# Small matmuls of an RWKV scan and a retention mixer, ordered by tile form and row half instead of in turns

## The chip, the cores and the metric

The kernel runs on one core of one Trainium2 chip. The metric is the device time of one execution in microseconds. The kernel before takes 2054.99 us (median of three runs, 2052.9 to 2055.63).

## The reference, cut to what matters

Two layers of a decoder work on a prompt of 512 tokens and on eight samples of four tokens each; both share the weights (`D_MODEL = 1024`). In each layer one large projection of the normalised input feeds four mixers and their gates; the mixers' results are merged, projected and added; then comes a feed-forward part. Two of the four mixers hold the change:

```python
# retention, chunks of 128 tokens, 4 heads of 64
s = jnp.einsum('bihd,bjhd->bhij', qb, kb) * dmask
o = jnp.einsum('bhij,bjhe->bihe', s, vb)
o = o + jnp.einsum('bihd,hi,bhde->bihe', qb, q_dec, S)
S = S * c_dec[None, :, None, None] + jnp.einsum('bjhd,hj,bjhe->bhde', kb, k_dec, vb)

# RWKV-7, 4 heads of 64, token by token
S = (S * wt[:, :, None, :]
     + jnp.einsum('bhij,bhj->bhi', S, at)[..., None] * bt[:, :, None, :]
     + vt[..., :, None] * kt[..., None, :])
y = jnp.einsum('bhij,bhj->bhi', S, rt)
```

For the samples the state comes in from memory, one per sample.

## The kernel before, in words

Features lie on the 128 partitions and the 544 tokens along the free axis, in two halves of 272. Nearly all weights stream from memory in units of 128 x 1024; each is split into a rounded part and a rest (ScalarE at line 109, VectorE at line 110), and each product is three matmuls (`mm3`, lines 129 to 131). These unit matmuls, 128 x 128 weights against 272 columns, are by far the largest part of the work of TensorE.

The mixers with small matmuls are generators (`rwkv`, `retention`). The program advances them by a step after each unit of weights (`tick`), so that their work stands between the unit matmuls. The code's order is not quite the order in which an engine runs its instructions: when the program is built, a scheduler puts each engine's instructions in order, by their place in the code among those whose inputs and buffers it holds ready. From then on each engine runs its list in order.

Heads of 64 features come in pairs: `p` is the pair, `q` the head within it. `par_rows(q)` are the partitions 0 to 63 or 64 to 127, and `kv_rows(q)` are the other half. The pieces that matter:

- *The scan of the prompt* (lines 587 to 628): 16 steps of 32 tokens in each layer, so 32 in all. A step makes `psG` (line 597), multiplies it by a triangular inverse (`ginv_sa`, line 577), and copies the result into the two halves of the state tile `Z`: `Z[0]` on VectorE (line 579), then `Z[1]` on ScalarE (line 580). Then come, for each of four pairs of `p` and `q`, a matmul into `psP` (line 604: 64 rows, 64 columns, with the row half `kv_rows(q)`) and one into `psY` (line 606: 128 rows, 64 columns). From `psP` VectorE and GpSimd make the next state (lines 612 to 621); every fourth step `psY` is copied out.
- *The samples of the scan* (lines 633 to 642): for each `p`, 16 matmuls of 64 x 64 weights against 8 columns into `psG0` (line 640), first the eight samples of one row half, then those of the other.
- *The retention* (from line 704, `def retention`), once for each `p` of each layer: scores of four chunks in two PSUM tiles, one for each `q` (line 720: 64 rows, 128 columns), masked on VectorE (line 723); products of keys and values (line 730) and their running sums `Sb` on VectorE; the output in `psO` (lines 742 and 744), where each chunk and head has one matmul from the masked scores (128 x 64) and, from the second chunk on, one from the state (64 x 64); and the samples (lines 765 and 767), where each `q` has one matmul from its scores (32 x 64) and eight of 64 x 64 from the samples' states.

PSUM tiles of these parts come from a pool of five banks (`psm`); the unit matmuls have three of their own.

Of the kernel before, what the change touches and what calls it, by code (L numbers as in the profile page):

```python
# [18 lines left out]
NB = 8  # L19
# [23 lines left out]
def tile_hybrid_step(ctx: ExitStack, tc: tile.TileContext, io: dict):  # L43
# [51 lines left out]

# [1 line left out]
    wloaded = {}  # L97
# [44 lines left out]

# [1 line left out]
    sgc = ZR(256)  # L144
# [13 lines left out]
    def ada_first(k):  # L158
        """feature tile k of the first norm's shift and scale; the four row groups sum every fourth 128 rows."""
        ps = PM()  # L160
        raw, sb = raws[k], sbs[:, 256 * k:256 * k + 256]
        for i in range(2):
            for kk in range(8):
                n = kk % 4
                PE.matmul(ps[32 * n:32 * n + 32, 128 * i:128 * i + 128], lhsT=sc[:, kk, :],
                          rhs=raw[:, 1024 * i + 128 * kk:1024 * i + 128 * kk + 128], start=(kk < 4), stop=(kk >= 4))
        S.copy(sb, ps[:, 0:256])
        yield
        for i in range(2):
            PE.matmul(ps[:, 256 + 9 * i:265 + 9 * i], lhsT=sb[:, 128 * i:128 * i + 128], rhs=cst[:, C_STK:C_STK + 9],  # L170
                      start=True, stop=True)
        V.tensor_tensor(
            out=mods[0].rearrange("p (s k) j -> p s k j", k=8)[:, 0:2, k, :],
            in0=ps[:, 256:274].rearrange("p (s j) -> p s j", s=2),
            in1=pars[0][:, P_BADA:P_BADA + 16].rearrange("p (s k) -> p s k", k=8)[:, :, k:k + 1].broadcast_to([128, 2, 9]),
            op=ADD)
        scales(0, (1,), slice(k, k + 1))
        yield

    def ada(l, sec, ns, load):  # L180
        """ns sections of the conditioning; a row group holds a fourth of their columns."""
        W = 256 * ns
        ps = PM()
        nxt = load(0)
        yield
        for k in range(8):
            raw = nxt
            if k < 7:
                nxt = load(k + 1)
            for n in range(4):  # L190
                PE.matmul(ps[32 * n:32 * n + 32, 0:W], lhsT=sc[:, k, :], rhs=raw[:, W * n:W * n + W], start=(k == 0), stop=(k == 7))  # L191
            yield
        sb = ZR(W)
        S.copy(sb, ps[:, 0:W])
        pt = PM()
        for q in range(2 * ns):
            PE.transpose(pt[:, q * 128:(q + 1) * 128], sb[:, q * 128:(q + 1) * 128], ident)
        V.tensor_tensor(
            out=mods[l][:, 8 * sec:8 * sec + 8 * ns, :].rearrange("p (n q) j -> p n q j", q=2 * ns),
            in0=pt[:, 0:W].rearrange("p (q n j) -> p n q j", q=2 * ns, n=4)[:, :, :, 0:9],  # L200
            in1=pars[l][:, P_BADA + 8 * sec:P_BADA + 8 * sec + 8 * ns].rearrange("p (n q) -> p n q", q=2 * ns).unsqueeze(3)
            .broadcast_to([128, 4, 2 * ns, 9]), op=ADD)
        scales(l, range(sec, sec + ns), slice(0, 8))
        yield
# [27 lines left out]

# [1 line left out]
    def xk(xt, k):  # L234
        return xt[k // 4][:, k % 4, :]

    def sum_sq(acc, x):
        """acc + x * x over the features seen so far."""
        sq = ZR(x.shape[1])
        S.activation(sq, x, AF.Square)  # L240
        if acc is None:
            return sq
        V.tensor_tensor(out=acc, in0=acc, in1=sq, op=ADD)
        return acc

    def rstd_of(accs):
        """(mean + eps) ** -0.5 of tokens, on every partition: taken with a token a partition, then spread."""
        n = HALF // 4
# [50 lines left out]
    def both_halves(run, norm):  # L299
        """eight output tiles, the first half's tokens and then the second's; a half's norm goes beside what follows."""  # L300
        ng = None
# [29 lines left out]

# [1 line left out]
    def par_rows(par):  # L333
# [5 lines left out]
    def ln_bones(src_halves, n, scale, bias, out, floor=None):  # L339
        """out = log(scale * blocksum(src) + bias) over 64-feature heads; exp_half makes it the sum's power -1/2."""  # L340
        for c0, c1 in ((0, HALF), (HALF, TOK)):
# [15 lines left out]
    def rwkv(l, za, zb, M, yD):  # L357
# [46 lines left out]
        def products(T):  # L404
            """the chunk's cumulative decays, and with them its scaled rows into LG and its scaled keys"""
            n = 128 if T < 4 else 32
# [33 lines left out]
        for T in range(5):  # L440
# [29 lines left out]
            yield  # L470
        # gate and bonus
        for p in range(2):
# [10 lines left out]
        yield  # L483
        # unit triangular inverses by substitution, a block (and row parity) a partition
        scr1 = drp.tile([64, 32, 32], F32, tag="scr1", name=nm("scr1"))
# [12 lines left out]
        nc.sync.dma_start(X, io["xinit"])  # L498
        # inverse of the samples' 4x4 blocks: (I + N)(I + N^2)
        psA2 = PM()  # L500
# [86 lines left out]
        for T in range(4):  # L587
            psY = PM()
            pY = psY[:, 0:256].rearrange("p (q x) -> p q x", q=2)
            for c in range(4):  # L590
# [10 lines left out]
                for p in range(2):  # L601
                    for q in range(2):
                        r = kv_rows(q)
                        PE.matmul(psP[par_rows(q), 64 * p:64 * p + 64], lhsT=BK[r, ch, p, :], rhs=Z[q][r, c % 2, p, :],  # L604
                                  start=True, stop=True)
                        PE.matmul(pY[par_rows(q), p, 32 * c:32 * c + 32], lhsT=Z[q][:, c % 2, p, :], rhs=LG[q][:, ch, p, 32:64],  # L606
                                  start=True, stop=True)
# [19 lines left out]
        G.dma_start(io["o_wkv_p"][l], Pn)  # L627
        # samples
        P0 = [ZR(512) for _ in range(2)]
# [4 lines left out]
        for p in range(2):  # L634
            if p:
                yield
            for q in range(2):
                r = par_rows(q)
                for b in range(NB):
                    PE.matmul(g0v[r, p, :, b, :], lhsT=P0[p][r, 64 * b:64 * b + 64],  # L640
# [34 lines left out]
        yield  # L675
        # group norm, bonus, gate
        rss = []
# [24 lines left out]

# [1 line left out]
    def retention(l, p, rt, M, yB):  # L704
# [10 lines left out]
        sms = []  # L715
        for q in range(2):
            r = par_rows(q)
            ps = PM()
            for T in range(4):
                PE.matmul(ps[:, 128 * T:128 * T + 128], lhsT=rt[r, 1, 128 * T:128 * T + 128],  # L720
                          rhs=rt[r, 0, 128 * T:128 * T + 128], start=True, stop=True)
            sm = ZR(512)
            V.tensor_tensor(out=sm.rearrange("j (T i) -> j T i", T=4), in0=ps.rearrange("j (T i) -> j T i", T=4),
# [14 lines left out]
        for T in range(4):  # L738
            for q in range(2):
                r = par_rows(q)  # L740
                oo = psO[r, 128 * T:128 * T + 128]
                PE.matmul(oo, lhsT=vt[:, T, r], rhs=sms[q][:, 128 * T:128 * T + 128], start=True, stop=(T == 0))  # L742
                if T:
                    PE.matmul(oo, lhsT=Sb[r, T, :], rhs=rt[r, 0, 128 * T:128 * T + 128], start=False, stop=True)  # L744
        S.copy(o[:, 0:SEQ], psO)
# [17 lines left out]
        for q in range(2):  # L763
            r = par_rows(q)
            PE.matmul(psO2[r, 0:32], lhsT=vks[32 * q:32 * q + 32, 0:64], rhs=sms_s[32 * q:32 * q + 32, :], start=True, stop=True)
            for b in range(NB):
                PE.matmul(psC[r, 4 * b:4 * b + 4], lhsT=S0[r, 64 * b:64 * b + 64], rhs=rt[r, 0, SEQ + 4 * b:SEQ + 4 * b + 4],
# [27 lines left out]
    def pad_evac(fn, dst, ps, half, pad):  # L795
        """write a half's tokens behind their past columns: fn(out, in)."""
        if half == 0:
# [7 lines left out]
    def first_units(k):  # L805
        """row tile k of the first three units, so that they run while the conditioning still arrives."""
        xh, xl = hh[k // 4][:, k % 4, :], hh[2 + k // 4][:, k % 4, :]
# [4 lines left out]

    # ================= program =================
    xs_dram = drp.tile([128, 8, TOK], F32, tag="xs", name="xs")
# [41 lines left out]
    for l in range(L):  # L856
# [80 lines left out]

# [1 line left out]
        yC = T4(F32R)  # L939
# [52 lines left out]

# [1 line left out]
        acc = []  # L994
        mix = None

        def gates(ys, first, last, hooks=()):
            """merge one branch; its projection runs a tile behind its gate, and hooks[m] after gate tile m."""
            nonlocal ui, mix
# [42 lines left out]

# [1 line left out]
        yA = T4(F32R)  # L1044
# [48 lines left out]

# [1 line left out]
        adv(rw, 2)  # L1095
# [48 lines left out]

# [1 line left out]
        wctx = ExitStack()  # L1146
# [26 lines left out]

# [1 line left out]
        fctx = ExitStack()  # L1175
# [109 lines left out]

# [1 line left out]
def _constants():  # L1287
# [197 lines left out]
```

## Time and profile before

| | |
|---|---|
| median of the timed runs | 2054.99 us (2052.9 to 2055.63, three runs) |
| span of the profiled execution | 2060.2 us |
| TensorE matmul busy (PE) | 98% of the span |
| TensorE weight load busy (PEld) | 92% |
| VectorE (DVE), ScalarE (ACT), GpSimd (POOL) busy | 51%, 40%, 15% |
| memory traffic | 227.23 MB, 110 GB/s on average |
| mean granted TensorE clock | 0.983 |

A line of the profile names a line of the code (L604), the engine, the operation, the tile written and the tiles read, and the form as rows x columns of the weights. Durations of matmuls are modelled and overlap each other, so that a group's busy time is no price; the chain of work that ended last gives each piece only the time that it adds. The granted clock is the share of TensorE's clock that the throttle let through. The profiled execution is one more execution beside the three timed ones.

### The profile page before, as it was taken

Reading aid. Unit: us, or ns where it says so; the run is one execution under the profiler, and the core shown is the slowest. Engines: PE = TensorE matmul, PEld = TensorE weight load, DVE = VectorE, ACT = ScalarE, POOL = GpSimd, SP = SyncE. Lnnn points to the kernel's source line nnn. Section 1 sums busy time; section 2 is a strip of 40 time slices with the busy share of each in tenths; the row PEclk is TensorE's granted clock in tenths of the full one; section 3 lists DMA queues with packets and bytes.
Section 4 is the critical chain, followed back from the end, with each engine's and each line's share of the span. In section 5 each row is a group of like instructions: output and inputs, shape, how many; then the busy total and the mean of one; then the engine's idle time right before and its main releaser. Section 6 shows DMA issues by size and latency. Waiting matters only on the chain.

```text
span 2060.2 us, 40148 instructions
## 1 busy us (share of the span) xinstructions
PE 2028.6 (98%) x16868; PEld 1897.2 (92%) x16868; DVE 1052.8 (51%) x2017; ACT 830.6 (40%) x1546; POOL 318.7 (15%) x589
## 2 busy tenths in 40 slices
PE   6999999999999999999999999999999999999998
PEld 5999988888999999999999999887899999999997
DVE  4465523353457553555663655333434666545565
ACT  5553322243336542434354533222533465333542
POOL 1110122212001220112202101222130012011210
PEclk9999999999999999999999999989999999999999
DMA  7224323232343443534322223123123322222221
GB/s 299 103 73 134 106 93 124 82 129 103 135 155 103 164 160 124 205 123 164 128 102 94 73 83 86 57 69 96 69 78 126 110 73 92 83 93 83 93 92 53
DMA packets 75557, 227.23 MB, mean 110 GB/s; under 512 B 20208, under 2 KB 23072, under 8 KB 73584
## 3 DMA queue, kind: packets, MB, share of 16 engines
q1 hardware_dynamic: 69872, 210.43, 29.9%
q0 software_dynamic: 3536, 11.53, 1.6%
q10 hardware_dynamic: 1968, 2.69, 0.5%
q8 instruction: 133, 2.18, 0.4%
q14 instruction: 48, 0.39, 0.1%
HBM read 213.33 MB, written 9.06 MB: 108 GB/s over the span
## 4 chain that ended last, share of the span: by engine, by line
PE 96%; DVE 2%; ACT 1%; DMA 0%; issue 0%; SPq 0%; DVEq 0%; ACTq 0%
PE pd L129 28%; PE pd L131 27%; PE pd L130 27%; PE pm L191 2%; PE pm L604 2%; PE pm L606 1%; PE pm L597 1%; PE pm L577 1%; DMA t<-in_wada 0%; PE pm L563 0%; PE pm L453 0%; PE pm L742 0%; PE pm L343 0%; PE pm L744 0%; DVE wlo L110 0%; PE pm L461 0%
## 5 line engine op out<-in xcount | busy, mean ns | idle before, releaser
L129 PE MATMUL pd<-t,whi 128*128 128x272 f32 x4200 | 1234.2, 294 | 5.2 <-ACT t L354 4.0
L131 PE MATMUL pd<-t,wlo 128*128 128x272 f32 x4200 | 1227.5, 292 | 0.0
L130 PE MATMUL pd<-t,whi 128*128 128x272 f32 x4200 | 1220.0, 291 | 0.6 <-DVE t L355 0.6
L129 PEld LDWEIGHTS pd<-t,whi 128*128 128x128 f32 x4200 | 795.9, 190 | 50.4 <-issue 34.7
L130 PEld LDWEIGHTS pd<-t,whi 128*128 128x128 f32 x4200 | 798.6, 190 | 7.5 <-issue 3.4
L131 PEld LDWEIGHTS pd<-t,wlo 128*128 128x128 f32 x4200 | 798.3, 190 | 4.4 <-issue 1.7
L110 DVE TENSOR_TENSOR wlo<-raw,whi 128x1024 fp32r<-128x1024 f32 x262 | 321.9, 1229 | 303.1 <-ACT whi L109 302.5
L109 ACT CAST whi<-raw 128x1024 fp32r<-128x1024 f32 x264 | 276.6, 1049 | 493.2 <-PE pd L130 456.8
L1196 POOL COPY off<-zr 128x18 f32<-128x18 f32 x88 | 77.0, 875 | 570.3 <-ACT zr L1194 570.3
L1016 DVE TENSOR_TENSOR zr<-pd,zr 128x272 f32<-128x272 f32 x96 | 41.6, 438 | 183.2 <-PE pd L131 183.0
L323 DVE SCALAR_TENSOR_TENSOR t<-pd,mod,t 128x272 f32<-128x272 f32 (+1 forms) x160 | 76.8, 482 | 112.1 <-PE pd L131 111.6
L1031 ACT ACTIVATE zr<-pd 128x272 f32<-128x272 f32 x128 | 50.4, 395 | 153.1 <-PE pd L131 148.8
L1194 ACT COPY zr<-pd 128x272 f32<-128x272 f32 (+2 forms) x264 | 72.7, 311 | 94.8 <-PE pd L131 94.8
L1017 POOL TENSOR_TENSOR t<-t,zr 128x272 f32<-128x272 f32 x64 | 73.2, 1160 | 218.3 <-DVE zr L1016 218.1
L945 DVE SCALAR_TENSOR_TENSOR zr<-zr,par,zr 128x560 f32<-128x560 f32 x92 | 73.5, 801 | 4.7 <-ACT zr L944 4.7
L946 DVE SCALAR_TENSOR_TENSOR zr<-zr,par,zr 128x560 f32<-128x560 f32 x92 | 73.5, 801 | 2.9
L944 ACT ACTIVATE zr<-zr,par 128x560 f32<-128x560 f32 x92 | 70.5, 766 | 7.6
L355 DVE TENSOR_TENSOR t<-zr,t 128x544 fp32r<-128x544 f32 (+1 forms) x96 | 54.0, 581 | 31.0 <-ACT t L354 30.1
L240 ACT ACTIVATE zr<-t 128x272 f32<-128x272 f32 (+1 forms) x72 | 32.1, 454 | 86.7 <-DVE t L323 54.5
L354 ACT CAST t<-zr 128x544 fp32r<-128x544 f32 (+1 forms) x96 | 48.9, 531 | 43.4 <-DVE zr L1207 42.0
L614 DVE TENSOR_TENSOR pt<-pm,pn 128x128 f32<-128x128 f32 x30 | 8.8, 292 | 70.7 <-PE pm L604 66.5
L604 PE MATMUL pm<-z,t 64*64 64x64 f32 x256 | 42.2, 246 | 0.0
(286 smaller groups left out, 1788.4 us busy)
## 6 DMA issues: line engine op xcount, KB each, us to landing
raw<-in_wst SPq DMA_DIRECT2D x276, 512.0 KB, 3.5
t<-in_wada SPq DMA_DIRECT2D x32, 1024.0 KB, 7.6
raw<-in_wada SPq DMA_DIRECT2D x32, 512.0 KB, 3.5
zr<-in_rope POOLq DMA_DIRECT2D x16, 272.0 KB, 3.2
t<-in_xT SPq DMA_DIRECT2D x4, 544.0 KB, 6.7
zr<-zr ACTq DMA_DIRECT2D x32, 68.0 KB, 4.3
t<-in_xT SPq DMA_DIRECT2D x2, 1088.0 KB, 8.3
xs<-t SPq DMA_DIRECT2D x2, 1088.0 KB, 4.4
```

Source lines behind the costliest of these rows:

```text
L109: S.copy(hi, raw)
L110: (G if (l, u) in ((0, 1), (0, 2)) else V).tensor_tensor(out=lo, in0=raw, in1=hi, op=SUB)
L129: PE.matmul(ps, lhsT=a, rhs=xh, start=first, stop=False)
L130: PE.matmul(ps, lhsT=a, rhs=xl, start=False, stop=False)
L131: PE.matmul(ps, lhsT=b, rhs=xh, start=False, stop=last)
L323: V.scalar_tensor_tensor(out=x[:, c0:c0 + npc], in0=ps[:, :npc], scalar=gate[:, m, 0:1], in1=x[:, c0:c0 + npc], op0=MUL, op1=ADD)
L604: PE.matmul(psP[par_rows(q), 64 * p:64 * p + 64], lhsT=BK[r, ch, p, :], rhs=Z[q][r, c % 2, p, :], start=True, stop=True)
L945: V.scalar_tensor_tensor(out=cv, in0=u[:, 1:561], scalar=wcol(1), in1=cv, op0=MUL, op1=ADD)
L946: V.scalar_tensor_tensor(out=cv, in0=u[:, 2:562], scalar=wcol(2), in1=cv, op0=MUL, op1=ADD)
L1017: (V if last else G).tensor_tensor(out=a[:, c0:c1], in0=a[:, c0:c1], in1=gs, op=ADD)
L1194: pad_evac(lambda o, i, sl: S.copy(o, i), u, ps, half, 2)
L1196: G.tensor_copy(off[:, 22 * s + j], u[:, 512:562].rearrange("p (x t) -> p x t", t=2)[:, 0:25:3, :])
```

## The change

Five groups of matmuls are put in another order. The instructions themselves stay the same, with their operands; comments and docstrings are taken out as well, line for line.

- Scan step: the four matmuls into `psP` come first, then the four into `psY`, instead of one of each in turns.
- Samples of the scan: the loop over the two row halves is now inside the loop over the samples.
- Scores of the retention: both PSUM tiles are taken at the start, and the two row halves take turns.
- Output of the retention: first all matmuls from the scores, then all from the state. Only the first chunk's matmul of each half has `start=True`; the others write into columns that nothing has been added to.
- Samples of the retention: first the two matmuls of 32 rows, then those of 64 rows with the row halves in turns.

```diff
@@ scan step
                         PE.matmul(psP[par_rows(q), 64 * p:64 * p + 64], lhsT=BK[r, ch, p, :], rhs=Z[q][r, c % 2, p, :],
                                   start=True, stop=True)
+                for p in range(2):
+                    for q in range(2):
                         PE.matmul(pY[par_rows(q), p, 32 * c:32 * c + 32], lhsT=Z[q][:, c % 2, p, :], rhs=LG[q][:, ch, p, 32:64],
                                   start=True, stop=True)
@@ samples of the scan
-            for q in range(2):
-                r = par_rows(q)
-                for b in range(NB):
+            for b in range(NB):
+                for q in range(2):
+                    r = par_rows(q)
                     PE.matmul(g0v[r, p, :, b, :], lhsT=P0[p][r, 64 * b:64 * b + 64],
...
@@ scores of the retention
-        for q in range(2):
-            r = par_rows(q)
-            ps = PM()
-            for T in range(4):
-                PE.matmul(ps[:, 128 * T:128 * T + 128], lhsT=rt[r, 1, 128 * T:128 * T + 128],
+        pss = [PM(), PM()]
+        for T in range(4):
+            for q in range(2):
+                r = par_rows(q)
+                PE.matmul(pss[q][:, 128 * T:128 * T + 128], lhsT=rt[r, 1, 128 * T:128 * T + 128],
                           rhs=rt[r, 0, 128 * T:128 * T + 128], start=True, stop=True)
+        for ps in pss:
             sm = ZR(512)
...
@@ output of the retention
         for T in range(4):
             for q in range(2):
                 r = par_rows(q)
-                oo = psO[r, 128 * T:128 * T + 128]
-                PE.matmul(oo, lhsT=vt[:, T, r], rhs=sms[q][:, 128 * T:128 * T + 128], start=True, stop=(T == 0))
-                if T:
-                    PE.matmul(oo, lhsT=Sb[r, T, :], rhs=rt[r, 0, 128 * T:128 * T + 128], start=False, stop=True)
+                PE.matmul(psO[r, 128 * T:128 * T + 128], lhsT=vt[:, T, r], rhs=sms[q][:, 128 * T:128 * T + 128],
+                          start=(T == 0), stop=(T == 0), skip_group_check=True)
+        for T in range(1, 4):
+            for q in range(2):
+                r = par_rows(q)
+                PE.matmul(psO[r, 128 * T:128 * T + 128], lhsT=Sb[r, T, :], rhs=rt[r, 0, 128 * T:128 * T + 128],
+                          start=False, stop=True, skip_group_check=True)
@@ samples of the retention
             PE.matmul(psO2[r, 0:32], lhsT=vks[32 * q:32 * q + 32, 0:64], rhs=sms_s[32 * q:32 * q + 32, :], start=True, stop=True)
-            for b in range(NB):
+        for b in range(NB):
+            for q in range(2):
+                r = par_rows(q)
                 PE.matmul(psC[r, 4 * b:4 * b + 4], lhsT=S0[r, 64 * b:64 * b + 64], rhs=rt[r, 0, SEQ + 4 * b:SEQ + 4 * b + 4],
```

## The prediction, made before the result was known

> **What bounds the kernel now.** First the page: span, busy time by engine, then the chain that ended last.
>
> ```profile
> span 2060.2 us, 40148 instructions
> ...
> PE 2028.6 (98%) x16868; PEld 1897.2 (92%) x16868; DVE 1052.8 (51%) x2017; ACT 830.6 (40%) x1546; POOL 318.7 (15%) x589
> ...
> PE 96%; DVE 2%; ACT 1%; DMA 0%; issue 0%; SPq 0%; DVEq 0%; ACTq 0%
> ```
>
> TensorE is busy nearly all the time, and 96% of the chain runs through it. So a microsecond taken out of TensorE's stream is worth about 0.96 us, as long as the stream has something else to run. A busy TensorE need not be a quick one, though: what one instruction costs is read from the chain in order of time, where each piece ends where the next begins. Here is one scan step of layer 0 (start, duration, what; every fp32 matmul leaves two records, so "x2" is one matmul of the code).
>
> ```profile
> 235.71 0.34 PE pm L597 x6
> ...
> 236.88 0.34 PE pm L577 x8
> ...
> 237.92 0.25 PE pm L604 x2
> 238.17 0.23 PE pm L606 x2
> 238.41 0.26 PE pm L197
> 238.67 0.26 PE pm L604 x2
> 238.92 0.23 PE pm L606 x2
> ```
>
> L577 runs eight records of one form in 0.34 us. L604 (a 64x64 tile) and L606 (128x64) alternate, and there two records already take 0.25 and 0.23 us, about three times as much a record. The rows of L604 and L606 in the list by form say how often:
>
> ```profile
> L604 PE MATMUL pm<-z,t 64*64 64x64 f32 x256 | 42.2, 246 | 0.0
> L606 PE MATMUL pm<-t,z 128*64 128x32 f32 x256 | 39.2, 236 | 0.0
> ```
>
> 256 records each are 128 matmuls each, four in each of 32 scan steps. What the same 64x64 form costs when its row halves take turns without another form between them, the chain shows at L453 and L461, 32 records each:
>
> ```profile
> 130.97 1.08 PE pm L453 x32
> 132.05 0.93 PE pm L461 x32
> ```
>
> L461 follows its own form: 0.93 / 32 = 0.029 us a record. L453 comes after a 128x128 form: 0.15 us more, the price of entering the form. These two numbers carry most of the sum. The other groups that are reordered, and the end of the scan's code beside them:
>
> ```profile
> 388.31 1.64 PE pm L720 x16
> ...
> 397.82 1.75 PE pm L640 x32
> ...
> 400.14 0.62 PE pm L730 x16
> 400.76 0.43 PE pm L742 x6
> 401.19 0.36 PE pm L744 x2
> 401.55 0.36 PE pm L742 x2
> ```
>
> L640 is the form of L461, but one row half at a time: 1.75 / 32 = 0.055 us a record, nearly twice L461's 0.029. L730 (128x64, the two column halves in turn) takes 0.62 us for 16.
>
> **The change, part by part.** No instruction is added or dropped, and no DMA is moved, so no queue of SP or POOL sees another order of its own work; what changes is the order of matmuls within TensorE's groups, and when their results are ready.
>
> *Scan (32 steps).* Before: 4 x (0.25 + 0.23) = 1.92 us a step. With four L604 and then four L606 in one piece each: 0.15 + 8 x 0.029 = 0.38 us, and about 0.36 us for eight of 128 rows (L577's eight take 0.34, half of L730's sixteen plus an entry 0.38): 0.74 us, 1.18 saved. I don't expect one piece each. In the step above a foreign matmul (L197) stands behind the first L604 and L606: the second L604 needs the scan state's other half, which is copied a little later. In the changed order the first L604 is followed by one that isn't ready; the first L606 is ready, then comes the filler, then the remaining three L604 and three L606. L597 already shows such a split, with its x6 in 0.34 us. So: 0.25 + 0.23 + 0.34 + 0.34 = 1.16 us, 0.76 saved, x 32 = 24.3 us. Bounds: 37.8 us (32 x 1.18) in whole groups, and nothing if the instructions end up alternating anyway.
>
> *Retention output (four times: two layers, two head pairs).* L742 has 16 records, L744 twelve. Before: 0.43 + 5 x 0.36 + 6 x 0.36 = 4.39 us. After: 16 in the six's pace (0.43 / 6 = 0.07, of which the last is unpaired) 1.0 to 1.15 us, twelve with an entry 0.8 to 1.0 us; 1.9 together. 2.5 saved, x 4 = 10.0 us. L744 also waits for running sums of the state on VectorE; behind all of L742 it is later, so these are readier than before.
>
> *Sample loop of the scan (L640, four times).* 1.75 becomes 0.15 + 32 x 0.029 = 1.08 us: 0.67 x 4 = 2.7 us.
>
> *Sample loop of the retention (L767, four times).* For the first head pair of a layer it is cut in two by L765, another form:
>
> ```profile
> 420.11 0.23 PE pm L765 x2
> 420.34 1.02 PE pm L767 x16
> 421.36 0.23 PE pm L765 x2
> 421.58 1.17 PE pm L767 x16
> ```
>
> 2.65 us become 0.23 + 1.08 = 1.31, 1.3 saved, twice; where it is in one piece I take L640's 0.67, twice. Together 3.9 us.
>
> *Scores (L720, four times).* 16 records at 0.103 us, one half after the other. Side by side eight pairs at about 0.107 and an entry: 1.0 us; 0.6 x 4 = 2.4 us. Both PSUM banks must now be free before the first matmul; the row shows all sixteen in one piece, so both were held then too, and I price this at nothing (a late bank would put unit matmuls in front, which are due anyway). The masks on VectorE start some 0.5 us later for the first half; TensorE has unit matmuls to run meanwhile.
>
> Sum of the matmuls: 24.3 + 10.0 + 2.7 + 3.9 + 2.4 = 43.3 us.
>
> *The clock.* Four stretches hold all these groups, and in each the granted clock (the figure behind the five engines' busy times) is below 1:
>
> ```profile
> 230.00:390.00 160.00, 159.94 (x1404) 133.50 (x1403) 53.42 (x112) 42.41 (x101) 35.17 (x58) 0.96 0.26 87
> 390.00:500.00 110.00, 109.96 (x923) 92.33 (x924) 45.73 (x74) 45.47 (x75) 21.83 (x25) 0.97 0.36 122
> 1260.00:1408.00 148.00, 148.00 (x1245) 126.04 (x1245) 47.84 (x98) 36.56 (x87) 35.38 (x54) 0.93 0.19 62
> 1408.00:1515.00 107.00, 105.99 (x841) 90.83 (x840) 42.16 (x69) 42.97 (x71) 24.00 (x28) 0.94 0.23 78
> ```
>
> 0.04 x 160 + 0.03 x 110 + 0.07 x 148 + 0.06 x 107 = 26.5 us of clock are lost there. In slices of 3.41 us:
>
> ```profile
> 282.39:285.80 3.41, 3.38 (x29) 2.40 (x29) 0.29 (x1) 0.89 (x3) 0.80 (x2) 1.00 0.78 286
> 285.80:289.21 3.41, 3.41 (x16) 3.35 (x16) 2.18 (x4) 0.65 (x1) 0.51 (x1) 0.50 0.07 26
> 289.21:292.62 3.41, 3.41 (x29) 3.41 (x29) 0.00 (x0) 0.40 (x1) 0.00 (x0) 1.00 0.43 154
> ```
>
> The slice that starts at 282.39 holds a whole run of L604 and L606 and hardly a large matmul; the next one is granted half the clock and gets 16 matmuls instead of 29, a loss of 13 x 0.12 = 1.6 us. The scan's two stretches lose 16.8 us, about ten such slices. There are 32 steps and only some ten slow slices, so a run of L604 and L606 is near the edge of what brings one. With the run 0.76 us shorter, six more large matmuls (3.41 / 29 = 0.12 us each) fit into its slice, and most should stay on the full side. I take 15 of the 26.5 us back. Ends: 25 (all of it), and 5 lost if the denser small groups bring three new slow slices.
>
> The Trainium skill ("TensorE: Matmul & The Clock Gate", Part 1) says that the gate halves the clock after an idle window of about 3.4 us. The length agrees with the slices here; that the window must be idle does not, for TensorE stands as busy 3.38 of 3.41 us before the slow slice. Read by busy time the rule would leave this term at nothing and the time at 2013.
>
> *Cover.* VectorE and ScalarE are busy for a third of the scan's stretches or less and DMA for about a quarter, so weights keep up with a TensorE that is 10% quicker there. For what ends on other engines I take the chain's 96%: (43.3 + 15) x 0.96 = 56 us. The profiled execution's span of 2060.2 us becomes 2004; it lies 5.2 us above the median of the three timed runs, 2054.99, which becomes **1999**.
>
> **The rivals.**
>
> *Whole groups.* If the state's other half counts as ready in time, the scan saves 37.8 instead of 24.3 us and more of the clock returns (20): (43.3 + 13.5 + 20) x 0.96 = 74 us, 1981. For it: the state's second half is copied within 0.58 us of the first (rows below), little more than the 0.48 that the first two matmuls take. Against: the filler in the step above.
>
> *The clock stays.* The gate counts something that the shorter runs don't change; busy time is the same in slow and full slices. 43.3 x 0.96 = 42 us, 2013.
>
> *Row halves don't overlap into one bank.* L604, L640, L744 and L767 write both row halves into one PSUM bank. If these run in turn, at 0.055 us a record (L744, with twice the columns, at 0.103): scan 0.25 + 0.23 + 0.48 + 0.34 = 1.30, 19.8 saved; L640 nothing; L767 1.3; L744 and L742 2.0 x 4 = 8; L720, on two banks, 2.4. With 10 of clock 41.5 x 0.96 = 40 us, 2015. L453 and L461 write one bank from both row halves too, and their 0.029 speaks against it. The Trainium skill ("TensorEngine Tiling (Array Packing)", Restrictions and Gotchas, Gotcha 1) states that different row tiles can't use the same bank at once; in this trace they do, on disjoint partitions.
>
> *The order isn't followed.* Engine order is planned when the program is built, by what is ready, and the scan's matmuls become ready one by one. If the scan alternates as before, only the loops whose inputs all stand ready gain: 19.0 + 5 of clock, x 0.96 = 23 us, 2032.
>
> *Slower: TensorE stalls within the step.* TensorE takes its stream in order. If the plan puts the four L604 close together on a modelled time at which the second half isn't copied yet, TensorE stands, with L606 and all unit matmuls queued behind. The copies:
>
> ```profile
> 258.93 0.29 DVE L579 COPY z<-pm 32x128 f32<-32x128 f32 x1 [0.95 <-PE pm L577]
> ...
> 259.25 0.26 ACT L580 COPY z<-pm 32x128 f32<-32x128 f32 x1 [0.83 <-DVE z L579]
> ```
>
> From the first copy's start to the second's end are 0.58 us, 18.6 over 32 steps. That alone doesn't eat 43.3. It does if each stall also brings a slow slice: 1.6 us in each of the 22 steps that have none now, 35 us; 43.3 - 18.6 - 35 = -10, 2065. It turns the sign once some 20 of the 32 steps pay 0.58 + 1.6. Against: L604 rarely waits now, since fillers stand ahead of it, and these stay.
>
> **How the numbers follow.** Forecast 0.50, whole groups 0.17, clock stays 0.17, no overlap 0.04, order not followed 0.08, stall 0.025, nothing measurable 0.015. About 0.2% (4 us) can be told from no change; every case but the last two is faster by more. The range, 1972 to 2027: its lower end is whole groups with all the clock ((43.3 + 13.5 + 25) x 0.96 = 79, and some 4 us for entries that the fillers need no more), its upper end the scan at half its saving and 2 us of clock lost ((12.2 + 19.0 - 2) x 0.96 = 28); outside lie the order not followed and the last two.
>
> **What would show it.** In the chain of the changed kernel L604 and L606 should stand as x2, x2, then x6, x6 (or x8, x8) with under 1.2 us a step; L742 x16 and L744 x12 in pieces, L640 and L767 x32 at 1.1 us, L720 x16 at 1.0. The granted clock of the four stretches should be 0.98 or more. Wrong would be: 0.055 us a record in alternating halves; the same number of slow slices; idle time ahead of L604 put down to the copies of L579 and L580; or a chain that leaves TensorE for more than 4%.

## The result, and the profile after

The changed kernel takes 2000.16 us (median of four runs, 1997.68 to 2001.29) against 2055.31 us before (four runs, 2052.9 to 2065.68). The ratio is 0.9719, with a 95% interval from 0.9691 to 0.9746. The forecast was 1999 us, in a range from 1972 to 2027.

The page of the kernel after: span, busy time by engine, and the chain by engine.

```profile
span 1995.9 us, 40151 instructions
...
PE 1962.4 (98%) x16868; PEld 1850.0 (93%) x16868; DVE 1047.5 (52%) x2017; ACT 829.4 (42%) x1546; POOL 318.8 (16%) x589
...
PE 95%; DVE 2%; ACT 1%; DMA 1%; issue 0%; ACTq 0%; SPq 0%; DVEq 0%
```

TensorE is as full as before, with the same 16868 matmul records; the span is shorter by what they took. The same scan step as in the prediction, in the chain of the kernel after (start, duration, what; L604 has kept its line, L606 is now L608):

```profile
239.12 0.26 PE pm L604 x2
239.37 0.23 PE pm L608 x2
239.60 0.26 PE pm L197
239.86 0.37 PE pm L604 x6
240.23 0.35 PE pm L608 x6
240.58 0.26 PE pm L197
```

The pieces are x2, x2, the filler, x6, x6, as forecast: 0.26 + 0.23 + 0.37 + 0.35 = 1.21 us instead of 1.92. In the trace 30 of the 32 steps have this form; the other two have whole groups.

The retention and the sample loops in the chain of the kernel after (L722 are the scores, L642 the samples of the scan, L744 and L749 the output; L771 and L775 the samples of the retention):

```profile
372.64 1.09 PE pm L722 x16
...
381.58 1.03 PE pm L642 x32
...
383.18 0.62 PE pm L733 x16
383.80 0.88 PE pm L744 x16
384.67 0.80 PE pm L749 x12
385.48 0.88 PE pm L642 x32
```

```profile
399.91 0.23 PE pm L771 x4
400.14 1.03 PE pm L775 x32
```

The output takes 0.88 + 0.80 = 1.68 us instead of 4.39. The second L642 has no entry to pay, since it follows L749, which has its form. And the four stretches that hold these groups, with the granted clock behind the five busy times:

```profile
230.00:372.00 142.00, 140.13 (x1392) 118.30 (x1391) 52.66 (x112) 41.14 (x99) 33.09 (x54) 1.00 0.30 100
372.00:465.00 93.00, 92.96 (x895) 79.57 (x894) 40.41 (x69) 40.34 (x70) 22.75 (x27) 1.00 0.40 134
1227.00:1358.00 131.00, 131.00 (x1305) 113.75 (x1303) 49.12 (x107) 40.22 (x98) 35.41 (x54) 1.00 0.23 70
1358.00:1465.00 107.00, 105.49 (x945) 94.96 (x944) 47.09 (x77) 50.17 (x81) 26.97 (x30) 0.98 0.28 92
```

Before they stood at 0.96, 0.97, 0.93 and 0.94. In this execution a single slow slice (one at half clock) is left in them, behind the retention's samples at 1441 us.

Single executions differ by the clock that they were granted, so times are also compared at one clock here. The kernel before ran 27 times beside the experiments, from 2050.76 us at a mean granted clock of 0.989 to 2071.06 at 0.980. A straight line through the 27 gives 1.86 us for each 0.001 of clock, and 2044.2 us at 0.993, the kernel after's usual clock. Their median is 2058.9 us at 0.985. So of the roughly 58 us between the kernels in these runs, about 44 are there at equal clock and about 15 are clock (8 x 1.86). This is an estimate, for none of the 27 executions had 0.993, and the line is drawn on past them.

### The profile page after: what moved, and what is told of

Read it like the earlier page. It is cut to its first block, busy times and chain, and to the rows that moved or that the text cites. A ratio compares the mean times of both kernels' runs of the same rounds, so it can differ in the third digit from the quotient of the medians.

```text
span 1995.9 us, 40151 instructions
## 1 busy us (share of the span) xinstructions
PE 1962.4 (98%) x16868; PEld 1850.0 (93%) x16868; DVE 1047.5 (52%) x2017; ACT 829.4 (42%) x1546; POOL 318.8 (16%) x589
## 4 chain that ended last, share of the span: by engine, by line
PE 95%; DVE 2%; ACT 1%; DMA 1%; issue 0%; ACTq 0%; SPq 0%; DVEq 0%
PE pd L129 28%; PE pd L131 27%; PE pd L130 27%; PE pm L191 2%; PE pm L604 1%; PE pm L608 1%; PE pm L597 1%; PE pm L577 1%; DMA t<-in_wada 1%; PE pm L453 0%; PE pm L563 0%; PE pm L343 0%; PE pm L165 0%; PE pm L461 0%; PE pm L672 0%
## 5 line engine op out<-in xcount | busy, mean ns | idle before, releaser
L1200 POOL COPY zr<-sff 128x16 f32<-128x16 f32 x88 | 41.0, 476 | 0.7 <-DMA sff<-in_s_ffn 0.4
L1211 ACT ACTIVATE zr<-zr 128x560 f32<-128x560 f32 x44 | 29.6, 672 | 24.9 <-DVE zr L954 24.9
```

## The experiments

**The scan step alone, and all but the scan step.** The first is the kernel before with this edit, the second the kernel after without it:

```diff
                                   start=True, stop=True)
+                for p in range(2):
+                    for q in range(2):
                         PE.matmul(pY[par_rows(q), p, 32 * c:32 * c + 32], lhsT=Z[q][:, c % 2, p, :], rhs=LG[q][:, ch, p, 32:64],
```

> The kernel before with the scan step alone reordered (four L604, then four L606). Theory (order costs TensorE time by itself, the clock is a smaller share): the two lines' own time falls from 63.5 to about 38 us as in the changed kernel, and of the ten slow slices in the scan's stretches hardly one stays; the slow slices of the sample stages (near 422, 1426 and 1446 us in the profile before) stay. 26 plus 6 to 10 us, 2020 to 2025 us. Rival (the gain is the clock's above all, and either part alone lifts it): the time comes within 10 us of the changed kernel, 2000 to 2010.

> The changed kernel with the scan step's order of before, so that only the retention's output and scores and the two sample loops are reordered. Theory: 18.5 us of matmul time plus 3 to 6 us of clock in the sample stages, 2030 to 2035 us; the slow slices in the scan's stretches stay. The savings of this run and of the scan alone add up to the whole within 5 us. Rival (the clock's part is common to both): they add up to clearly more or less than 55 us.

The scan alone took 2031.42 us (ratio 0.9856, 0.9826 to 0.9886), the rest alone 2025.38 us (0.9837, 0.9804 to 0.987). Both expected times missed, in opposite directions: the scan brought less and the rest more. Against the kernel before beside them (2060.33 us) they save 28.9 and 35.0 us, 63.9 together. The whole change saved 55.2 in its own runs and 61.4 in a later set, so this alone doesn't settle whether the parts add within 5 us. Moved along the line to a clock of 0.993 they are 2019.1 and 2026.3 us, savings of 25.1 and 17.9 us, which add up to 43.0 against the whole change's 44. What differed is the clock, a median of 0.9865 with the scan alone and 0.9935 with the rest alone. How far the line carries is shown by the next pair of profiles. The rival of the first run, 2000 to 2010 us, falls.

**Where the slow slices lie.** The kernel before and the scan alone were each profiled again, unchanged.

> The kernel before, unchanged, for a second look at where its slow slices lie. Theory (the slices depend on how the free-running 3.41 us grid falls on the stages): again 30 to 50 us at half clock between the first and the last microseconds, but at other steps of the scan; those of the sample stages come back at the same stages. Rival (they are tied to the instructions): the same ten or so places as in the first profile.

> The scan step alone reordered, for a second look at its slow slices. Theory A (each stage's slices depend on that stage's own matmuls): few in the scan's stretches (under 14 us at half clock), 20 us or more in the sample stages. Theory B (the first profile's split between the stages was chance): more in the scan than in the sample stages.

They took 2058.65 and 2026.03 us. The second execution of the scan alone had a clock of 0.993 and is still 7 us above the 2019.1 that the line gives, so the line is no better than that for this kernel. The four stretches of the kernel before, second profile, and then of the scan alone, second profile:

```profile
230.00:388.00 158.00, 156.98 (x1393) 130.59 (x1392) 52.75 (x111) 42.34 (x101) 34.28 (x56) 0.97 0.26 86
388.00:500.00 112.00, 111.95 (x943) 94.08 (x939) 45.99 (x76) 46.49 (x76) 23.23 (x27) 0.97 0.36 120
1255.00:1406.00 151.00, 151.00 (x1315) 128.47 (x1309) 51.10 (x106) 40.85 (x98) 37.02 (x57) 0.95 0.19 61
1406.00:1515.00 109.00, 107.87 (x853) 92.79 (x853) 43.39 (x71) 45.59 (x72) 22.91 (x25) 0.94 0.27 84
```

```profile
230.00:374.00 144.00, 141.63 (x1405) 119.51 (x1406) 52.74 (x112) 42.38 (x102) 34.16 (x56) 1.00 0.30 98
374.00:480.00 106.00, 105.95 (x895) 88.21 (x894) 43.59 (x71) 40.61 (x69) 22.09 (x26) 0.97 0.35 119
1240.00:1373.00 133.00, 132.25 (x1310) 114.50 (x1309) 49.62 (x108) 41.40 (x99) 35.81 (x55) 1.00 0.22 69
1373.00:1480.00 107.00, 105.67 (x842) 91.24 (x841) 42.10 (x69) 42.91 (x71) 23.93 (x27) 0.94 0.24 80
```

With the scan reordered its own two stretches stand at 1.00 and those of the samples stay at 0.97 and 0.94, so theory A holds. The first profile of the scan alone has 10.2 us at half clock in the scan's stretches, at one place, and 27.3 in the others. In the kernel before, the scan's part varies: 34.1 us at half clock in the first profile, 23.9 in the second. Of these 23.9 us, 17.1 stand in the same steps as in the first profile (one slice at 285 us, four in a row from 1351 and 1347 us) and the rest in others, so that neither the theory nor its rival holds as it stands. The samples' part is 20.5 us in both and stands at the same three stages. The profile of the rest alone, its execution with the lowest clock (0.990), shows the mirror image:

```profile
232.00:388.00 156.00, 155.17 (x1390) 129.16 (x1390) 52.50 (x111) 42.04 (x101) 33.71 (x55) 0.98 0.26 87
388.00:480.00 92.00, 91.56 (x886) 78.41 (x883) 40.96 (x67) 39.02 (x67) 21.25 (x26) 1.00 0.41 135
1242.00:1396.00 154.00, 154.00 (x1319) 130.89 (x1319) 52.69 (x108) 41.86 (x99) 35.67 (x56) 0.93 0.18 60
1396.00:1485.00 89.00, 87.67 (x815) 77.55 (x814) 40.68 (x68) 39.94 (x67) 21.40 (x25) 1.00 0.28 92
```

Each stage's slow slices come from that stage's own matmuls, with one exception. The scan alone has 10.2 us at half clock from 344.9 us on, the kernel after's second run 10.2 us from 342.9 us on, and these follow a pause of TensorE. Here are that run's slice with the pause (3.41 us long, TensorE busy for 1.86) and the one behind it, at half clock, and the wait that made the pause:

```profile
339.48:342.89 3.41, 1.86 (x21) 1.34 (x21) 2.89 (x6) 0.45 (x2) 0.81 (x1) 1.00 0.44 154
342.89:346.31 3.42, 3.42 (x27) 2.82 (x28) 0.29 (x1) 0.26 (x1) 0.00 (x0) 0.50 0.76 219
```

```profile
PE pm L597 <- DVE z L622: 1.6, 1, 1.6
```

Every kernel with the quicker scan waits near this place (1.6 to 3.0 us idle in one piece); the kernel before doesn't, or waits 1.0 us. In the four profiles where one slice held 1.5 us or more of the wait (scan alone, kernel after again, and two of the variants below, the output in turns and the halves in blocks), slow slices followed. In the first profile of the kernel after and the second of the scan alone a border of the slices, counted on from their slow ones, cuts the wait (1.24 and 0.56, 1.22 and 0.78 us), and none followed. Between these it went either way: none behind 1.49 us with the late half first at both lines, one behind 1.23 us with the late half first (both below).

The profiles also give a second estimate of what the order alone saves. A microsecond at half clock costs at most half a microsecond; with that taken off the spans for the four stretches' slow slices, the kernel before stands at 2032.9 and 2034.3 us, the scan alone at 2011.1 and 2014.0, the rest alone at 2017.3, and the kernel after at 1994.2 and 1992.1. These are savings of 21 and 16 us for the parts and 40 for the whole. They add within 3 us, which is also what two profiles of one kernel differ by.

**As many microseconds of small matmuls, but in dense groups.** This tells whether length or alternation brings the slow slices. The products are the same, written over again:

```diff
-                for p in range(2):
+                for p in [0, 1] * 3:
                     for q in range(2):
                         r = kv_rows(q)
                         PE.matmul(psP[par_rows(q), 64 * p:64 * p + 64], ...
-                for p in range(2):
+                for p in [0, 1] * 2:
                     for q in range(2):
                         PE.matmul(pY[par_rows(q), p, 32 * c:32 * c + 32], ...
```

> The changed kernel, but each scan step issues its four L604 three times and its four L608 twice (the same products written over again), so that the small matmuls of a step last about as long as before, 1.9 us, without alternating forms. 24 more records a step at 0.029 us: 0.70 us, 22 us over 32 steps. Theory C (a slice turns slow when too much of it goes to small matmuls, whatever their order): the slow slices of the scan come back, 7 to 14 us more, 2029 to 2037 us. Theory D (it is the alternating forms, in which the array stands empty, that bring them; dense small matmuls count as work): the granted clock stays at 0.993, 2020 to 2025 us.

It took 2019.6 us (ratio 0.9826, 0.9795 to 0.9857), at a median clock of 0.995. One step in its chain, and the scan's two stretches:

```profile
258.55 0.25 PE pm L604 x2
258.81 0.23 PE pm L608 x2
259.04 0.55 PE pm L191 x2
259.59 0.84 PE pm L604 x22
260.42 0.58 PE pm L608 x14
```

```profile
230.00:382.00 152.00, 150.15 (x1777) 128.47 (x1777) 51.28 (x110) 42.34 (x101) 34.60 (x56) 1.00 0.28 89
1236.00:1381.00 145.00, 145.00 (x1704) 126.76 (x1704) 50.37 (x109) 41.68 (x99) 35.83 (x56) 1.00 0.22 65
```

A step spends 0.25 + 0.23 + 0.84 + 0.58 = 1.90 us on small matmuls, as before the change, and no slice of the scan is slow. Theory D holds, for all four executions' clocks (0.993 to 0.996, against 0.979 to 0.989 of the kernel before) and for the time, which lies just under its 2020 us: in the scan dense small matmuls keep the clock, and it is not the length of a step's small matmuls that loses it. Most of the alternation is what the run takes away; that something else goes with it (how much of the array works in each microsecond, say) is not ruled out.

**The order of the halves in the scan.** First blocks of two instead of turns:

```diff
-                for p in range(2):
-                    for q in range(2):
+                for q in range(2):
+                    for p in range(2):
```

> The changed kernel, but in the scan step both L604 of one row half come first and then both of the other, and the same for the two column halves of L608 (this also lets the ready half run first, so pieces of x4, x4, filler, x4, x4). Theory (taking turns between halves counts beside the form): a step's own time goes from 1.21 to about 1.44 us, 7 us more over 32 steps, 2005 to 2010 us. Rival (only the change of form counts, halves in turns bring nothing): no slower than the changed kernel, 1997 to 2002.

It took 1991.97 us (0.9666, 0.9637 to 0.9695), 8 us less than the kernel after instead of 7 more: the expectation failed. A step of it in order of time, TensorE alone (durations overlap; the next start counts):

```profile
247.70 0.46 PE L604 MATMUL pm<-z,t 64*64 64x64 f32 x8
248.09 0.43 PE L608 MATMUL pm<-t,z 128*64 128x32 f32 x8
248.45 0.39 PE L131 MATMUL pd<-t,wlo 128*128 128x272 f32 x1
```

The groups came out whole: while both L604 of the half that is ready run, the other becomes ready, and 26 of 32 steps have x8, x8. And the whole groups take 0.39 + 0.36 = 0.75 us here (up to 0.84 in other steps), not much more than in turns (0.73, below), though the halves stand in blocks of two. So at this length the order of the halves hardly counts, and most of the gain is the entry into the form that no longer falls due twice: all matmuls of L604 and L608 together take 29.8 us where the kernel after has 37.7.

Then turns, but beginning with the half that is copied last:

```diff
-                    for q in range(2):
+                    for q in (1, 0):
```

> The changed kernel, but in the scan step the row half whose state is copied last comes first in both groups, so that all eight matmuls are ready when the first is and the groups stay whole (x8, x8). Theory: a step's own time goes from 1.21 to 0.73 us in some 29 steps, 14 us, and the filler needs no entry of its own, 3 to 5 us more: 1981 to 1986 us. Rival (the first matmul now waits for the second copy, 0.58 us after the first, and TensorE stands): idle time ahead of L604 of up to 0.5 us a step eats the gain, 1995 to 2005 us.

It took 1981.86 us (0.9613, 0.9584 to 0.9642), as the theory said. All 32 steps have whole groups. TensorE's waits for the second copy are 1.2 us in one place, as the list of waits shows:

```profile
PE pm L604 <- ACT z L580: 1.2, 1, 1.2
```

Done at L597 as well:

> As the run with the late half first, and L597 in that order too, so that its four matmuls are ready together. Some 13 steps no longer split L597: 0.2 us of entry each, and a filler's entry of 0.2: 3 to 5 us less than with the late half first, 1976 to 1980 us. Rival (L597's filler only moves ahead of it, and TensorE waits for the second half): the same, 1981 to 1984.

It took 1979.43 us (0.9623, 0.9599 to 0.9646). A step in its chain:

```profile
237.58 0.38 PE pm L604 x8
237.95 0.35 PE pm L608 x8
```

The step's 0.73 us are nearly the prediction's price of whole groups, 0.74. Against the run before it the gain is 2.4 us between two separate sets of runs on two chips (1978.4 to 1980.1 against 1979.2 to 1983.1): under the expected 3 to 5, and not told apart from nothing. Only six steps fewer split L597 (three against nine), not some 13.

**Parts of the rest, undone.** With the kernel after run again beside them.

```diff
# the sample loops: halves in blocks of eight samples (the same at L775)
-            for b in range(NB):
-                for q in range(2):
-                    r = par_rows(q)
+            for q in range(2):
+                r = par_rows(q)
+                for b in range(NB):
```

> The changed kernel, but in the two sample loops (L642, L775) the eight samples of one row half come first and then those of the other; the forms still stand together. Theory (in a long group the row halves must take turns to overlap): each of the eight loops goes from 1.03 back to 1.75 us, 5.8 us, and the slow slices that stood behind L767 come back in part, up to 6 us: 2006 to 2012 us. Rival (as in the scan's blocks of two, the order of the halves hardly counts): within 2 us of the changed kernel.

> The changed kernel with the retention's output alone as before (the two forms in turns). Theory: 2.7 us more in each of four places, 10.8 us, and some of the slow slices of that stage, up to 5 us: 2010 to 2016 us. Rival (the output's matmuls wait for VectorE's sums and masks anyway): under 5 us, 2000 to 2005.

> The changed kernel once more, on the same chip as the two runs beside it: 1997 to 2002 us, no more than two slow slices between the first 40 and the last 30 us.

The kernel after took 1998.7 us again (1996.24 to 2004.0). Its profile has three slow slices in a row from 343 us on, one more than expected; they are those behind the pause of TensorE shown above. The sample loops in blocks took 2012.57 us (2003.95 to 2017.51), just past the expected range; at a clock of 0.993 it is 2007.8, some 5 to 8 us above the kernel after, and the rest is clock (0.987 to 0.994 from run to run, where the kernel after beside it had 0.992 to 0.997). Two of the loops in its chain, which stood at 1.03 and 0.88 us in turns:

```profile
381.54 1.75 PE pm L642 x32
...
386.15 1.60 PE pm L642 x32
```

Here the form stays the same, and only the halves differ. The profile of this run has one slow slice behind an L642 and one behind an L775, where the kernel after's second run has none. So slow slices also come behind loops without alternating forms, whose small matmuls run one row half at a time. Nor are groups in turns wholly free of them: the kernel after's only one in the four stretches, in its first profile, follows a slice with an L775 in turns, and so do those of the repeated products (466 us) and of the late half at L597 too (446 and 1422 us). The output in turns of forms took 2010.82 us, 12 us more than the kernel after, as expected, at a clock of 0.993.

## Why the prediction was right, point by point

*The bound.* TensorE's stream did set the time: the order's 40 to 44 us, by the two estimates, are the sum of the matmul terms (43.3) at nearly full worth. Whether 0.96 was the right factor is finer than they can tell.

*The matmul terms.* Scan 1.21 us a step where 1.16 was put: 1.92 - 1.21 = 0.71, x 32 = 22.7 us for 24.3. Output 4.39 - 1.68 = 2.71, x 4 = 10.8 for 10.0. L642 saves 0.72 for 0.67, in both loops (1.75 to 1.03, and 1.60 to 0.88 against the halves in blocks). The retention's samples 2.65 - 1.26 = 1.39 for 1.3 where L765 had cut them. Scores 1.64 - 1.09 = 0.55 for 0.6. The split into x2, x2, x6, x6 was forecast from the filler in the step of before, and it came.

*The clock.* The way was right, and the size roughly: 15 of the 26.5 us were to come back. The line gives about 15, but 11 for the result's own medians (55.2 less 44), and the profiles' half-clock time gives 26 for the two first profiles (54.6 and 3.4 us). So the close agreement of the total has luck in it, and two of the reasons were wrong. The prediction put 16.8 of the loss into the scan from one profile; the scan's slices vary from execution to execution, and it is the rest that brings back most in the timed runs (a median of 0.9935 with the rest alone; 0.986 or 0.987 with the scan alone, and 0.993 once). Why the scan alone lies so low in most of them is open in part: its two profiles place 37.5 and 20.5 us at half clock in the four stretches, and 10.2 of the difference follow the pause at 341 us. And it said that the run of small matmuls, being shorter, leaves room for six more large ones in its slice. The repeated products show that this isn't what counts: the run was as long as before and the clock stayed. What failed is that step's mechanism, not its sum.

The Trainium skill ("TensorE: Matmul & The Clock Gate", Part 1) says that the clock is set by how busy TensorE has been recently. If busy is read from the profile, the pause near 340 us agrees (1.86 of 3.41 us busy, then half clock) and the scan of before does not: alternating and dense groups look equally busy in the profile, and in the scan only the first lose the clock. What the gate counts stays open; no run here measures it.

*The rivals.* Whole groups did not come, but two other orders of the same loop brought them. Beginning with the late half gains what the rival said (1981 forecast, 1981.86 measured); blocks of halves, with whole groups in 26 steps, reach 1991.97. That the clock stays falls with the four stretches. Row halves do overlap into one bank: L642 in turns takes 1.03 us for 32 records that take 1.75 in blocks. The order was followed. The stall didn't come; even with the late half first the matmuls' own waits for the copy are 1.2 us.

*Cover.* VectorE, ScalarE and the weight stream kept up but for one place, which the prediction does not name. From 330 to 342.7 us the chain of the kernel after leaves TensorE:

```profile
330.09 0.73 ACT whi L109
...
334.00 5.06 DMA zr<-zr
...
342.07 0.50 DVE z L622
...
342.70 0.27 PE pm L597 x2
```

A DMA for the retention's inputs comes first, then VectorE's sum that needs it (line 1135), then the scan's next state (L622), for which TensorE, with unit matmuls until then, waits 1.8 us. With the late half first its waits for L622 are 3.2 us. This is what a still quicker scan meets, and, in the executions where the pause falls into one slice, it costs clock as well.

## What to carry to other kernels

Read the price of small matmuls from the chain, per record and per change of form, and compare it with a place in the same kernel where the form stays: here two records cost 0.25 us after another form and 0.06 after their own. Put matmuls of one form together, begin with the operand that is ready last, so that the whole group is ready when it starts, and let row halves take turns where the group is long. Then look at the granted clock of the stretch before and after, because here alternating forms cost a second time there, and look for pauses that the quicker stream has opened.

## What the runs showed of the hardware that was not expected

- What taking turns between row halves brings depends on the length of the group: in groups of four matmuls, blocks of two cost 0.75 to 0.84 us for a step's two groups against 0.73 in turns, while in groups of sixteen, blocks of eight cost 1.75 against 1.03.
- The granted clock falls with alternating forms at equal busy time and equal length: 1.92 us of alternating matmuls a step left the scan's stretches at 0.93 to 0.97, 1.90 us of dense ones at 1.00. One row half at a time in groups of sixteen (the sample loops in blocks) lost some of it too, without a change of form.
- A pause of TensorE of 1.5 us or more within one slice of 3.41 us was followed by slices at half clock in all four profiles that have one in the scan; where a border of the slices cut the same wait (1.24 and 1.22 us at most) none followed, though one followed 1.23 us in another variant. So the same wait can cost clock in one execution and none in the next.
- The time of one program moves with the clock it happens to be granted: 27 executions of the kernel before spread over 20.3 us, nearly all of it on a line of 1.86 us for each 0.001 of clock.
